# RoPE on half of each head: the load behind the first store waits for a point in VectorE's work

## The chip, the core and the metric

The kernel runs on one core of a Trainium2 chip. The metric is the device time of one execution in microseconds (us), as the median of several. A profile gives a second figure, the span: from the first to the last of the program's own instructions. The device time is longer than the span (162.1 against 160.3 us in the profiled run of the kernel before).

All runs told of here are fast, with a granted clock of 1.0. A ratio of two kernels is the mean time of one kernel's fast runs over the mean of the other's fast runs of the same rounds; it is therefore not quite the ratio of the medians that are quoted beside it.

## The reference

The input `x` is 16 x 512 x 16 x 64 in fp32, 33.55 MB. The first 32 of each head's 64 values are rotated with `cos` and `sin`; the other 32 pass through.

```python
x1, x2 = (x[..., :half_dim].copy(), x[..., half_dim:].copy())
...
rotated_first = x1[..., :half_dim // 2] * cos[..., :half_dim // 2] - x1[..., half_dim // 2:] * sin[..., :half_dim // 2]
rotated_second = x1[..., :half_dim // 2] * sin[..., :half_dim // 2] + x1[..., half_dim // 2:] * cos[..., :half_dim // 2]
return np.concatenate([rotated_first, rotated_second, x2], axis=-1).astype(np.float32)
```

All 33.55 MB have to be read and written once. That makes 67.1 MB of traffic.

## The kernel before

The data are cut into four tiles of 8.39 MB, each 128 partitions by 16 rows of 1024 values. Three tiles fit in a ring of three slots, so tile 3 reuses tile 0's slot. All large loads and stores go through one queue, that of SyncE (the sync queue). VectorE rotates a tile in place, in two halves of eight rows (`KC = 8`), each with two multiplications, a subtraction and an addition. The products with `sin` stand in PSUM, in one buffer of eight rows.

```python
load(0)
load(1)
load(2, 0, KC)
# ... the table of cos and sin is built ...

def rotate(t, lo, hi):
    # ... views of the tile and of the table ...
    nc.vector.tensor_mul(out=b_t, in0=x1, in1=s)
    nc.vector.tensor_mul(out=x1, in0=x1, in1=c)
    nc.vector.tensor_sub(...)
    nc.vector.tensor_add(...)

def turn(t):
    rotate(t, 0, KC)
    rotate(t, KC, K)
    return store(t)

turn(0)
load(2, KC, K)           # "the load behind the first store"
near = load(3, 0, KL)    # slot of tile 0: waits for store 0 to land
load(3, KL, K)
# ... store(1), from turn(1), is made to wait for `near` ...
turn(2)
turn(3)
```

The order at the DMA engines is: tile 0 in, tile 1 in, half of tile 2 in, store 0, the other half of tile 2 in, tile 3 in, stores 1, 2 and 3. In the profile these nine land in this order, at 22.96, 42.99, 52.76, 72.45, 81.94, 101.36, 120.72, 140.01 and 159.29 us (each on the last of the 16 engines).

Of the kernel before, what the change touches and what calls it, by code (L numbers as in the profile page):

```python
# [1 line left out]

# [4 lines left out]


@with_exitstack
def kernel(  # L10
    ctx: ExitStack,
    tc: tile.TileContext,
    x: bass.AP,
    cos: bass.AP,
    sin: bass.AP,
    out: bass.AP,
):
    nc = tc.nc
    fp32 = mybir.dt.float32
    P = 128  # L20
    B, S, H, D = x.shape
    Q = D // 4
    HF = D // 2



    K = 16
    T = B * S // (P * K)
    PB = S // K
    REP = P // PB  # L30
    R = H * D
    NS = 3
    KC = K // 2
    KL = 14

    xf = x.rearrange("b s h d -> (b s h d)").rearrange("(t p f) -> t p f", t=T, p=P)
    of = out.rearrange("b s h d -> (b s h d)").rearrange("(t p f) -> t p f", t=T, p=P)
    cosf = cos.rearrange("(p k) j -> p (k j)", k=K)
    sinf = sin.rearrange("(p k) j -> p (k j)", k=K)

    const_pool = ctx.enter_context(tc.tile_pool(name="const", bufs=1))
    b_pool = ctx.enter_context(tc.tile_pool(name="bp", bufs=1, space=bass.MemoryType.PSUM))


    ring = const_pool.tile([P, NS, K, H, D], fp32)
    stage = const_pool.tile([P, 2, K, HF], fp32)
    spun = const_pool.tile([P, 2 * K, Q], fp32)
    packed = const_pool.tile([PB, 2 * K, Q], fp32)
    table = const_pool.tile([P, 2, K, 2, Q], fp32)

    def rows(t, lo, hi):
        return ring[:, t % NS, lo:hi].rearrange("p k h d -> p (k h d)")

    def load(t, lo=0, hi=K):
        return nc.sync.dma_start(out=rows(t, lo, hi), in_=xf[t, :, lo * R : hi * R])

    def store(t, lo=0, hi=K):
        return nc.sync.dma_start(out=of[t, :, lo * R : hi * R], in_=rows(t, lo, hi))


    nc.vector.memset(stage[:, :, :, 0:Q], 0.0)  # L61
    spread = stage.rearrange("(j b) t k i -> j b t (k i)", b=REP)
    nc.gpsimd.dma_start(out=spread[:, 0, 0], in_=cosf)  # L63
    nc.gpsimd.dma_start(out=spread[:, 0, 1], in_=sinf)  # L64
# [7 lines that stand above are left out]
    PQ = PB // REP  # L72
    nc.vector.stream_shuffle(  # L73
        out=spun[:],
        in_=stage.rearrange("p t k j -> p (t k) j")[:, :, 0:Q],
        mask=[j % PQ * REP for j in range(PB)],
    )
    for q in reversed(range(REP)):
        n = PQ * (q + 1)
        nc.vector.tensor_copy(out=packed[0:n], in_=spun[q * PB : q * PB + n])  # L80

    for r in range(REP):
        nc.vector.tensor_copy(  # L83
            out=table[r * PB : (r + 1) * PB].rearrange("p t k c j -> p (t k) c j"),
            in_=packed.unsqueeze(2).to_broadcast((PB, 2 * K, 2, Q)),
        )
    C = table[:, 0].rearrange("p k c j -> p k (c j)")
    Sn = table[:, 1].rearrange("p k c j -> p k (c j)")

    def rotate(t, lo, hi):  # L90
        x1 = ring[:, t % NS, lo:hi, :, 0:HF]
        c = C[:, lo:hi].unsqueeze(2).to_broadcast((P, hi - lo, H, HF))
        s = Sn[:, lo:hi].unsqueeze(2).to_broadcast((P, hi - lo, H, HF))
        b_full = b_pool.tile([P, KC, H, HF], fp32, name="b_t")
        b_t = b_full[:, 0 : hi - lo]
        nc.vector.tensor_mul(out=b_t, in0=x1, in1=s)  # L96
        nc.vector.tensor_mul(out=x1, in0=x1, in1=c)  # L97
        nc.vector.tensor_sub(  # L98
            out=x1[:, :, :, 0:Q], in0=x1[:, :, :, 0:Q], in1=b_t[:, :, :, Q:HF]
        )  # L100
        nc.vector.tensor_add(  # L101
            out=x1[:, :, :, Q:HF], in0=x1[:, :, :, Q:HF], in1=b_t[:, :, :, 0:Q]
        )

    def turn(t):
        rotate(t, 0, KC)
        rotate(t, KC, K)
        return store(t)

    turn(0)  # L110
    load(2, KC, K)
    near = load(3, 0, KL)
    load(3, KL, K)

    tc.add_manual_dep(
        turn(1).ins,
        near.ins.name,
        mybir.DependencyInfo(mybir.DependencyClass.Sync, mybir.DependencyReason.DATA),
        reason="the store follows the loads at the DMA engines",
    )  # L120
    turn(2)
    turn(3)


# [1 line left out]
_INS = ['x', 'cos', 'sin']  # L126
_OUTS = [((16, 512, 16, 64), 'float32')]


# [23 lines left out]
```

## Time and profile before

| | before |
|---|---|
| device time, median of the first 3 runs | 161.58 us (161.43 to 161.9) |
| device time of the profiled run | 162.1 us |
| span of the profiled run | 160.3 us |
| bytes through the sync queue | 67.11 MB |
| VectorE busy | 112.4 us |

The prediction shows the windows of this profile, one for each transfer, and how to read them. In short: the DMA engines are never without work after the start (DMA share 0.99 to 1.02 in every stage from 22.1 us on), VectorE has slack (busy 112.4 of 160.3 us, none of it in the last stage).

### The profile page before, as it was taken

The numbers are of one execution on the slowest core, as the hardware profiler recorded it, in microseconds if no ns is written. First come the engines' busy times: TensorE is split into PE (matmuls) and PEld (weight loads), VectorE is DVE, ScalarE is ACT, GpSimd is POOL, SyncE is SP. The second block draws the span as 40 slices with busy tenths as digits, with TensorE's granted clock in tenths as the row PEclk, the third lists the DMA queues.
The fourth block names the chain that finished last, engine by engine and source line by source line (L and its number), as shares of the span: only waits on it lengthen the run. The fifth ranks groups of instructions, "written<-read, shape, count | busy, mean of one in ns | idle before, by whom it ended". The sixth has DMA issues, their size and how long they took to land.

```text
span 160.3 us, 113 instructions
## 1 busy us (share of the span) xinstructions
DVE 112.4 (70%) x43; POOL 1.4 (1%) x6
## 2 busy tenths in 40 slices
DVE  1000959999999999999999999999999950000000
POOL 3000000000000000000000000000000000000000
DMA  7969969699699996999999995996996996996990
GB/s 262 540 262 540 491 294 523 278 507 491 294 392 441 474 523 262 523 392 392 499 482 458 458 444 253 546 523 262 523 523 262 523 507 278 523 507 278 523 507 16
DMA packets 1504, 67.24 MB, mean 419 GB/s; under 512 B 192, under 2 KB 192, under 8 KB 224
## 3 DMA queue, kind: packets, MB, share of 16 engines
q1 hardware_dynamic: 1440, 67.11, 97.6%
q0 software_dynamic: 64, 0.13, 0.2%
HBM read 33.69 MB, written 33.55 MB: 419 GB/s over the span
## 4 chain that ended last, share of the span: by engine, by line
DVE 59%; DMA 14%; issue 7%; DVEq 1%
DVE b_t L96 22%; DVE ring L97 22%; DMA ring<-in_x_dram 14%; DVE ring L101 10%; DVE ring L98 4%; DVEq L148 1%; DVEq L96 0%
## 5 line engine op out<-in xcount | busy, mean ns | idle before, releaser
L96 DVE TENSOR_TENSOR b_t<-ring,table 128x4096 f32<-128x4096 f32 x8 | 35.5, 4432 | 2.1 <-DMA ring<-in_x_dram 1.9
L97 DVE TENSOR_TENSOR ring<-ring,table 128x4096 f32<-128x4096 f32 x8 | 35.4, 4424 | 0.3
L98 DVE TENSOR_TENSOR ring<-ring,b_t 128x2048 f32<-128x2048 f32 x8 | 18.3, 2287 | 0.3
L101 DVE TENSOR_TENSOR ring<-ring,b_t 128x2048 f32<-128x2048 f32 x8 | 18.2, 2280 | 0.0
L73 DVE LOAD_MASK_SELECT spun<-stage x1 | 0.0, 14 | 14.4 <-DMA stage<-in_sin_dram 14.4
L83 DVE COPY table<-packed 32x1024 f32<-32x1024 f32 x4 | 2.7, 684 | 0.1
L80 DVE COPY packed<-spun 32x512 f32<-32x512 f32 (+3 forms) x4 | 1.7, 416 | 0.1
L61 DVE MEMSET stage<- 128x512 f32 x1 | 0.5, 485 | 0.9 <-PEq L137 0.9
L73 DVE STREAM_SHUFFLE spun<-stage 128x512 f32<-128x512 f32 x1 | 0.7, 723 | 0.0
L63 POOL DMA_DIRECT2D stage<-in_cos_dram x1 | 0.6, 649 | 1.3 <-DVE stage L61 1.3
L64 POOL DMA_DIRECT2D stage<-in_sin_dram x1 | 0.5, 532 | 0.0
L137 POOL MEMSET const-float32-0.0<- 128x1 f32 x1 | 0.1, 93 | 0.2 <-issue 0.2
L137 POOL MEMSET const-bfloat16-1.0<- 128x1 bf16 x1 | 0.1, 95 | 0.0
L137 POOL MEMSET const-uint8-127<- 128x1 uint8 x1 | 0.1, 93 | 0.0
L137 POOL MEMSET const-float32-1.0<- 128x1 f32 x1 | 0.1, 92 | 0.0
## 6 DMA issues: line engine op xcount, KB each, us to landing
ring<-in_x_dram SPq DMA_DIRECT2D x2, 4096.0 KB, 41.4
ring<-in_x_dram SPq DMA_DIRECT2D x1, 7168.0 KB, 26.4
ring<-in_x_dram SPq DMA_DIRECT2D x1, 1024.0 KB, 28.5
stage<-in_cos_dram POOLq DMA_DIRECT2D x1, 64.0 KB, 9.0
stage<-in_sin_dram POOLq DMA_DIRECT2D x1, 64.0 KB, 13.4
out_dram<-ring SPq DMA_DIRECT2D x4, 25.6
ring<-in_x_dram SPq DMA_DIRECT2D x2, 32.0
```

What stands on the lines that cost most here:

```text
L61: nc.vector.memset(stage[:, :, :, 0:Q], 0.0)
L63: nc.gpsimd.dma_start(out=spread[:, 0, 0], in_=cosf)
L64: nc.gpsimd.dma_start(out=spread[:, 0, 1], in_=sinf)
L73: nc.vector.stream_shuffle(out=spun[:], in_=stage.rearrange("p t k j -> p (t k) j")[:, :, 0:Q], mask=[j % PQ * REP for j in range(PB)],)
L80: nc.vector.tensor_copy(out=packed[0:n], in_=spun[q * PB : q * PB + n])
L83: nc.vector.tensor_copy(out=table[r * PB : (r + 1) * PB].rearrange("p t k c j -> p (t k) c j"), in_=packed.unsqueeze(2).to_broadcast((PB, ...
L96: nc.vector.tensor_mul(out=b_t, in0=x1, in1=s)
L97: nc.vector.tensor_mul(out=x1, in0=x1, in1=c)
L98: nc.vector.tensor_sub(out=x1[:, :, :, 0:Q], in0=x1[:, :, :, 0:Q], in1=b_t[:, :, :, Q:HF])
L101: nc.vector.tensor_add(out=x1[:, :, :, Q:HF], in0=x1[:, :, :, Q:HF], in1=b_t[:, :, :, 0:Q])
L137: nc = _bacc.Bacc("TRN2", target_bir_lowering=False, num_devices=1)
L148: with _tile.TileContext(nc) as tc:
```

## The change

Behind store 0 the kernel issues the load of tile 2's second half. In the kernel before that load stands in the queue for 21 us while store 0 runs. The change issues it only near the store's end, by making it wait for VectorE to finish 11 of tile 1's 16 rows. To have a point at the right time, tile 1 is rotated in pieces of 6, 5 and 5 rows instead of 8 and 8. The other transfers keep their order and their waits.

```diff
-    turn(0)
-    load(2, KC, K)
-    near = load(3, 0, KL)
-    load(3, KL, K)
-    ...   # turn(1), its store waiting for `near`
-    turn(2)
-    turn(3)
+    rotate(0, 0, KC)
+    rotate(0, KC, K)
+    store(0)
+    rest = load(2, KC, K)
+    near = load(3, 0, KL)
+    load(3, KL, K)
+    rotate(1, 0, 6)
+    behind(rest, rotate(1, 6, 11))     # behind(): one more semaphore wait
+    rotate(1, 11, K)
+    behind(store(1), near)
+    for t in range(2, T):
+        rotate(t, 0, KC)
+        rotate(t, KC, K)
+        store(t)
```

(`rotate` now also returns its last instruction, so that a wait can name it.)

More of the change, by code (lines that the diff above doesn't have):

```diff
@@ L100, in rotate, with behind @@
         )
-        nc.vector.tensor_add(
+        return nc.vector.tensor_add(
             out=x1[:, :, :, Q:HF], in0=x1[:, :, :, Q:HF], in1=b_t[:, :, :, 0:Q]
         )
-    def turn(t):
+    def behind(transfer, point):
+        tc.add_manual_dep(
+            transfer.ins,
+            point.ins.name,
+            mybir.DependencyInfo(
+                mybir.DependencyClass.Sync, mybir.DependencyReason.DATA
+            ),
+            reason="issue the transfer near the end of the one in front of it",
+        )
+    rotate(0, 0, KC)
[9 more added lines that the diff above has]
+    for t in range(2, T):
         rotate(t, 0, KC)
         rotate(t, KC, K)
-        return store(t)
-    turn(0)
-    load(2, KC, K)
-    near = load(3, 0, KL)
-    load(3, KL, K)
-    tc.add_manual_dep(
-        turn(1).ins,
-        near.ins.name,
-        mybir.DependencyInfo(mybir.DependencyClass.Sync, mybir.DependencyReason.DATA),
-        reason="the store follows the loads at the DMA engines",
-    )
-    turn(2)
-    turn(3)
+        store(t)
 _INS = ['x', 'cos', 'sin']
```

## The prediction

> **What bounds the kernel now.** I read the page first, then the windows cut at the transfers' ends, then the issues and the sync queue's own waits, and last the timeline around the first store. The page, parts 1 and 3:
>
> ```profile
> DVE 112.4 (70%) x43; POOL 1.4 (1%) x6
> ...
> q1 hardware_dynamic: 1440, 67.11, 97.6%
> ```
>
> VectorE works 112.4 of 160.3 us; the sync queue's transfers fill 97.6% of what 16 DMA engines could do in the span. 67.11 MB is four tiles of 8.39 MB in and four out. The chain on the page is led by VectorE, but its last VectorE operation ends at 130.6 us and 28 us of pure storing follow, so I do not follow that chain: the DMA engines set the time. The windows, one for each stage of the traffic (tile 0 in; tile 1 in; first half of tile 2 in; store 0; second half of tile 2 in; tile 3 in; stores 1, 2, 3), with columns stretch, length, busy times, clock, DMA share, GB/s:
>
> ```profile
> 0.74:22.10 21.36, 5.62 (x11) 1.18 (x2) 1.00 0.95 399
> 22.10:42.30 20.20, 19.11 (x6) 0.00 (x0) 1.00 1.00 417
> 42.30:52.10 9.80, 9.73 (x4) 0.00 (x0) 1.00 1.01 431
> 52.10:71.40 19.30, 19.16 (x6) 0.00 (x0) 1.00 0.99 431
> 71.40:81.10 9.70, 9.63 (x4) 0.00 (x0) 1.00 1.02 438
> 81.10:100.46 19.36, 19.19 (x7) 0.00 (x0) 1.00 1.00 433
> 100.46:119.80 19.34, 19.20 (x7) 0.00 (x0) 1.00 1.02 441
> 119.80:139.10 19.30, 10.71 (x4) 0.00 (x0) 1.00 0.99 428
> 139.10:158.41 19.31, 0.00 (x0) 0.00 (x0) 1.00 0.99 431
> ```
>
> The reader is to see that transfers follow one another without a hole, and that from 52.1 us on each 8.39 MB takes 19.3 us, whether it is a load or a store and whether or not something is queued behind it. (A packet is counted whole where it starts, so single figures scatter by some GB/s around the true rate.) The rate is lower only before 52.1: the start costs about 2 us and tile 1's load runs at 417.
>
> Now the place of the change. The issues view, cut to the moment of the first store and of the load behind it (last column: us from issue to landing):
>
> ```profile
> ring<-in_x_dram SPq DMA_DIRECT2D x1, 4096.0 KB, 31.6
> out_dram<-ring SPq DMA_DIRECT2D x1, 22.5
> ```
>
> The store is issued at 49.94 and lands at 72.4; the load is issued at 50.33 and lands at 81.9, that is 9.5 us after the store, its own 4.19 MB at 441 GB/s. So they do not share the engines by turns: the load stands in line for 21 us and then runs. The sync queue's own waits, in the window from 49 to 75 us:
>
> ```profile
> SPq L58 <- DVE ring L101: 26.9, 1, 26.9
> SPq L55 <- DMA out_dram<-ring: 21.7, 1, 21.7
> ```
>
> The first is store 0 waiting for tile 0's rotation. The second is tile 3's load, which reuses tile 0's slot and so waits for store 0's landing. In these 21.7 us the sync queue has nothing to do: the new wait falls inside it.
>
> [...]
>
> **The change, part by part.** The order of instructions on the sync queue is the same; the load of tile 2's second half gets one more wait, on VectorE. VectorE does tile 1 in three pieces in place of two: 12 instructions instead of 8.
>
> *VectorE's added cost.* The work is split, not enlarged[...]. Tile 1 ends at 77.5 instead of 76.83, and the last rotation at 131.3 instead of 130.6. None of it reaches the end: store 1 waits for tile 3's load to land (98.8); store 2, issued at 103.7, would be issued at 104.4, and its turn comes at 119.8; store 3, issued at 131.3, has its turn at 139.1. The smallest slack is 7.8 us. Cost on the path: 0.
>
> *The point of issue.* From the timeline:
>
> ```profile
> 49.94 4.43 DVE L96 TENSOR_TENSOR b_t<-ring,table 128x4096 f32<-128x4096 f32 x1
> ...
> 63.39 4.43 DVE L96 TENSOR_TENSOR b_t<-ring,table 128x4096 f32<-128x4096 f32 x1
> ```
>
> Eight rows of tile 1 take 13.45 us, of which 13.42 are its four instructions. [...] With 0.03 each for gaps the first piece ends at 60.2 and the second at 68.86. The load is then issued at about 68.9 instead of 50.33. Store 0's data end at 71.4, so the load is 2.5 us early.
>
> *Is 2.5 us enough?* Windows at the first load of all and at the hand-over:
>
> ```profile
> 0.74:1.70 0.96, 0.48 (x1) 0.00 (x0) 1.00 0.00 0
> 1.70:2.70 1.00, 0.00 (x0) 1.00 (x2) 1.00 3.06 1049
> ...
> 68.80:69.80 1.00, 1.00 (x1) 0.00 (x0) 1.00 2.42 1049
> 69.80:71.30 1.50, 1.50 (x1) 0.00 (x0) 1.00 0.00 0
> 71.30:72.30 1.00, 0.98 (x1) 0.00 (x0) 1.00 1.22 524
> ```
>
> The first load was issued at 0.74; its packets started between 1.7 and 2.7 on all engines (1.05 MB, 16 packets of 64 KB), so 1 to 2 us from issue to work on a cold queue. The store's last 16 packets start between 68.8 and 69.8, and the load's first ones after 71.3. Issued at 68.9, the load is ready by 69.9 to 70.9, 0.4 to 1.4 us ahead of need: no hole, cost 0. Its landing stays at 81.9, 8.4 us before VectorE asks for it (90.28 in the timeline). Tile 3's load is still issued at store 0's landing, 72.5.
>
> *What could be gained.* If one transfer's waiting descriptors slow the one in front, store 0 should run below the stores that have nothing at their end. It does not: 19.30 us, against 19.34, 19.30 and 19.31. [...] All that is before 52.1 lies ahead of the point where the change begins.
>
> Sum: [...]0 for VectorE, 0 for the hand-over: 161.6 us, within the noise of the three runs before (161.43 to 161.9).
>
> **Rivals.** *A: a hole at the hand-over.* If queue start-up in mid-stream takes over 2.5 us, or the load's reads can no longer begin under the store's last writes, the engines stand idle. The cold start cost 1 us of no packets, and stage one took 21.4 us against 19.3, about 2 us over. For it: the lead is a single packet's time[...]. Against it: 2.5 us exceeds the cold start's 1 to 2[...]. It would make 162.0 to 163.5. I give it one chance in eight.
>
> *B: the queued load slows the store, so its delay helps.* For it: the change's author applies the same idea already to store 1, which waits for tile 3's load; and tile 1's load, with another behind it, ran at 417. Against it: tile 0's load had two behind it and store 0 one, and store 0 runs at full rate; tile 3's load had a further load behind it and took 19.4 with that. [...]
>
> *C: VectorE becomes the bound.* It gets 0.7 us later, against a slack of 7.8 us. It would need eleven times the cost. 161.6 unless that arithmetic is badly off.
>
> *D: the sync queue blocks.* It stands before the load until 68.9, where it stood before the next one until 72.5 in any case. Nothing else is issued between, so 161.6.
>
> **Range and chances.** The centre is the sum, 161.6. [...]upward the spread and the mild half of A, 162.3. Two per cent is 3.2 us. [...]slower by that would need a hole longer than the whole cold start. So 0.01, 0.97 and 0.02.
>
> **What would show each step right or wrong.** In the changed kernel the sync queue should wait for VectorE's line 101-equivalent a second time, about 18.5 us; the load's issue should stand near 68.9 and its time to landing fall from 31.6 to about 13.0 us; store 0's stay near 22.5; tile 3's load wait some 3 us for the store in place of 21.7; VectorE's busy time rise by 0.6 to about 113.0 us. In the windows, the stage of store 0 should still be 19.3 us and the next one start at once at 71.4. A stretch without packets between 71.4 and 72.4, with the landing later than 82, would be rival A. Store 0 landing 0.3 us or more earlier with everything behind it moved along would be B. I would be wrong altogether if the transfers before 52.1 changed, since nothing of the change reaches them by this reading.

The sum came to 161.6 us, with a range of 161.1 to 162.3.

What the traces give:

- The five full-tile stages after 52.1 us ran at 431, 433, 441, 428 and 431 GB/s, 433 in the mean. A 64 KB packet took 2.42 us in the median.
- Tile 3's load, which waits for store 0, was issued at 72.47 us, 0.02 us after the store's last landing (72.45). So the shown start of that issue is the end of its wait.
- The load's first packet starts at 71.40 us, while the store's last one runs to 71.78: the two overlap.
- An estimate, made from this profile after the fact: operations of 4096 elements a partition took 4.432 and 4.424 us, those of 2048 took 2.287 and 2.280. A straight line through their means has 1.047 ns for an element and 139 ns for an instruction, so four instructions more add 0.56 us. By the same estimate six rows take 10.21 us and five 8.60, and the point is reached at 68.81 us. In the changed kernel the two pieces took 10.24 and 8.64 us and the point was reached at 68.76 (the first piece began 0.06 us earlier).

## The result, and the profile after

| | before | changed |
|---|---|---|
| device time, median of 6 runs | 161.58 us (161.43 to 162.16) | 162.25 us (162.16 to 162.57) |
| ratio | 1 | 1.0036 (95%: 1.0019 to 1.0054) |
| span, profiled run | 160.3 us | 160.0 us |
| device time, profiled run | 162.1 us | 162.16 us |

The changed kernel is slower by 0.36%: 0.67 us between the medians. That counts as the same at the 2% mark, and lies in the predicted range, but it is clear of the noise and was not expected. And the two profiles seem to say the contrary: the changed kernel's span is shorter. So the first task is to find where 0.67 us can hide.

The page of the changed kernel, its head and VectorE's line:

```profile
span 160.0 us, 117 instructions
## 1 busy us (share of the span) xinstructions
DVE 112.9 (71%) x47; POOL 1.4 (1%) x6
```

VectorE has four instructions more and is busy 0.5 us longer (112.9 against 112.4; 0.6 was foreseen). The sync queue's own waits between 49 and 75 us (who waited for whom, total, times, longest):

```profile
SPq L58 <- DVE ring L101: 26.9, 1, 26.9
SPq L55 <- DVE ring L101: 18.5, 1, 18.5
SPq L55 <- DMA out_dram<-ring: 2.6, 1, 2.6
```

The new wait is the second line. The third is tile 3's load, which still waits for store 0 to land, but now for 2.6 us, where it was 21.7: the queue's waiting has only changed its name. The timeline gives the issue, and the issues view the time from issue to landing:

```profile
68.76 3.77 SPq L55 DMA_DIRECT2D ring<-in_x_dram  x3
```

```profile
ring<-in_x_dram SPq DMA_DIRECT2D x1, 4096.0 KB, 12.9
```

The load was issued at 68.76 and landed 12.9 us later, as foreseen (68.9 and 13.0). The windows of the changed kernel, one for each transfer as in the prediction (stretch, length, VectorE, GpSimd, clock, DMA share, GB/s):

```profile
22.00:41.35 19.35, 18.22 (x6) 0.00 (x0) 1.00 1.00 432
41.35:51.10 9.75, 9.68 (x4) 0.00 (x0) 1.00 1.01 434
51.10:70.42 19.32, 19.11 (x9) 0.00 (x0) 1.00 1.00 433
70.42:80.60 10.18, 10.08 (x5) 0.00 (x0) 1.00 1.02 414
80.60:99.98 19.38, 19.21 (x7) 0.00 (x0) 1.00 0.99 428
```

Two stages differ from the first profile of the kernel before. Tile 1's load (first line) took 19.35 us at 432 GB/s, where it had taken 20.20 at 417: 0.85 us won in a stage that ends long before the change begins. And the moved load (fourth line) took 10.18 us at 414, where it had taken 9.70 at 438: 0.48 us lost. The first lies ahead of all that the change touches, so it may be one run's chance; the second may be the change. This had to be tested, and so had the difference between device time and span: 2.16 us here, 1.8 before.

### The profile page after: what moved, and what is told of

The parts are those of the page before. It is cut to its first block, busy times and chain, and to the rows that moved or that the text cites. A ratio compares the mean times of both kernels' runs of the same rounds, so it can differ in the third digit from the quotient of the medians.

```text
span 160.0 us, 117 instructions
## 1 busy us (share of the span) xinstructions
DVE 112.9 (71%) x47; POOL 1.4 (1%) x6
## 4 chain that ended last, share of the span: by engine, by line
DVE 60%; DMA 14%; issue 7%; DVEq 1%
DVE b_t L96 22%; DVE ring L97 22%; DMA ring<-in_x_dram 14%; DVE ring L101 10%; DVE ring L98 5%; DVEq L156 1%; DVEq L96 0%
## 5 line engine op out<-in xcount | busy, mean ns | idle before, releaser
L96 DVE TENSOR_TENSOR b_t<-ring,table 128x4096 f32<-128x4096 f32 (+2 forms) x9 | 35.6, 3958 | 2.1 <-DMA ring<-in_x_dram 1.9
L97 DVE TENSOR_TENSOR ring<-ring,table 128x4096 f32<-128x4096 f32 (+2 forms) x9 | 35.6, 3950 | 0.3
L98 DVE TENSOR_TENSOR ring<-ring,b_t 128x2048 f32<-128x2048 f32 (+2 forms) x9 | 18.4, 2050 | 0.3
L101 DVE TENSOR_TENSOR ring<-ring,b_t 128x2048 f32<-128x2048 f32 (+2 forms) x9 | 18.4, 2042 | 0.0
```

The source lines that it names most:

```text
L98: nc.vector.tensor_sub(out=x1[:, :, :, 0:Q], in0=x1[:, :, :, 0:Q], in1=b_t[:, :, :, Q:HF])
L101: return nc.vector.tensor_add(out=x1[:, :, :, Q:HF], in0=x1[:, :, :, Q:HF], in1=b_t[:, :, :, 0:Q])
```

## The experiments

All twelve were correct and ran in three groups, with five rounds each beside the kernel before, which gave four to six fast runs of each kernel. Each group has its own controls; their median span was 159.8 us in all three. This table sums them up. "Span" is the median over all fast runs of that kernel. "Beyond" is the median of device time minus span. "Tail" is, in the profile, the span minus the landing of the last store (its issue plus its time to landing). "Last landing" is the median span less the tail: the end of the data traffic.

| kernel | device time | ratio | span | beyond | tail | last landing |
|---|---|---|---|---|---|---|
| before_again | 161.49 | 0.9992 | 159.7 | 1.80 | 1.04 | 158.7 |
| after_again | 162.21 | 1.0040 | 160.0 | 2.2 | 1.04 | 159.0 |
| split_no_wait | 161.97 | 1.0023 | 159.8 | 2.2 | 1.04 | 158.8 |
| wait_at_8_rows | 161.53 | 0.9999 | 159.75 | 1.8 | 1.04 | 158.7 |
| tiny4 | 161.90 | 1.0022 | 159.7 | 2.15 | 1.04 | 158.7 |
| wait_at_10_rows | 161.97 | 1.0024 | 159.8 | 2.2 | 1.04 | 158.8 |
| wait_at_12_rows | 163.08 | 1.0099 | 160.85 | 2.2 | 1.04 | 159.8 |
| tile3_later | 162.16 | 1.0038 | 160.4 | 1.8 | 1.35 | 159.05 |
| after_tiny4 | 162.21 | 1.0039 | 160.4 | 1.8 | 1.35 | 159.05 |
| tiny8 | 161.82 | 1.0018 | 160.1 | 1.8 | 1.35 | 158.75 |
| wait_at_mul | 161.75 | 1.0007 | 160.0 | 1.8 | 1.04 | 159.0 |
| head_early | 162.14 | 1.0036 | 159.9 | 2.2 | 1.1 | 158.8 |

Spans are recorded to 0.1 us, so differences of 0.1 in the last column mean nothing. The 95% intervals of the ratios are about 0.0013 wide on either side.

### The two kernels once more

`before_again` and `after_again` are the two kernels without an edit.

> The kernel before, unchanged, for a second profile and for the noise of a ratio. Every theory expects a ratio of 1.000 within 0.002. The point is the profile: in the first one tile 1's load ran at 417 GB/s (20.2 us), where in the changed kernel it took 19.35 us at 432. If that slowness belongs to the kernel before, it is there again (20.2 us); if it comes and goes by the run, this profile may show 19.4 us and a span some 0.8 us shorter than 160.3.

> The changed kernel, unchanged, in the same rounds as its controls. Every theory expects a ratio of about 1.004 (162.2 us). In the profile the stage of the load behind the first store should again take about 10.2 us in place of 9.7, if the lost half microsecond there is the kernel's and not that one run's.

Measured: 161.49 and 162.21 us, ratios 0.9992 and 1.0040. The difference is the kernel's. In the second profile of the changed kernel the moved load takes as long as in the first (10.18 us there):

```profile
70.49:80.75 10.26, 10.16 (x5) 0.00 (x0) 1.00 1.02 409
```

The windows of the second profile of the kernel before (tile 1 in, half of tile 2 in, store 0, the load behind it):

```profile
22.10:41.45 19.35, 18.23 (x6) 0.00 (x0) 1.00 1.00 435
41.45:51.15 9.70, 9.63 (x4) 0.00 (x0) 1.00 1.01 436
51.15:70.78 19.63, 19.49 (x6) 0.00 (x0) 1.00 1.00 426
70.78:80.62 9.84, 9.77 (x4) 0.00 (x0) 1.00 0.99 423
```

Tile 1's load took 19.35 us this time, so its slowness was one run's. (What slowed it stays open. One of the 11 control runs of the kernel before in this group took 162.12 us against 161.53 in the median, so such an execution is not unique, though that one has no trace.) And now store 0 and the load behind it, 19.63 and 9.84, take 0.47 us more than in the first profile (19.30 and 9.70). (These windows are cut where the first of the 16 DMA engines starts a transfer. To the landing on the last engine, 0.02 us after which the load that waits for store 0 was issued in the first profile, the second profile is only 0.15 us longer: 29.33 us from the landing of tile 2's first half to that of its second, against 29.18.) The kernel before, too, has slow packets where the store hands over to the load; the first profile happened to have none.

### Which part of the change costs: the split or the wait?

`split_no_wait`, from the changed kernel:

```diff
-    behind(rest, rotate(1, 6, 11))
+    rotate(1, 6, 11)
```

> Tile 1 in 6, 5 and 5 rows, without the new wait. Theory H (the load is issued too near the store's end, so its first packets run slowly at the hand-over): as before, ratio 1.000 within 0.002, the load's stage 9.7 us. Rival V (VectorE's 0.6 us of added work reaches the end): ratio 1.004.

`wait_at_8_rows`, from the changed kernel:

```diff
-    rotate(1, 0, 6)
-    behind(rest, rotate(1, 6, 11))
-    rotate(1, 11, K)
+    behind(rest, rotate(1, 0, KC))
+    rotate(1, KC, K)
```

> Tile 1 in two halves as before, with the wait, at the end of the first half: the load is issued at about 63.4 us, some 7 us before the store's data end. Theory H: 7 us is enough, ratio 1.000 within 0.002, stage 9.7 us. Rival W (a wait there costs in itself, whatever its point, through the sync queue or an added semaphore): ratio 1.004.

The wait without the split costs nothing (0.9999). That rules out rival W, a wait that costs in itself. The split without the wait costs 0.4 us (1.0023): theory H had expected 1.000 and missed. But its last store does not land later (158.8 against 158.7). So rival V, which has the longer chain of VectorE reach the end, is wrong as well: the time is lost after the span. Device time minus span is about 2.2 in every run of the changed kernel and of `split_no_wait`, and about 1.8 in every run of the kernel before and of `wait_at_8_rows`, which have the old number of instructions. What is there to see after the span? The DMA queues of `split_no_wait` between 159 and 165 us have one line:

```profile
q14 instruction: 1, 0.01, 0.5%
```

It is one packet of the queue that the profile names "instruction". In the trace it starts 1.7 us after the span's end. The first profile of the changed kernel has one as well: 8,192 bytes, started at 161.69 us and 0.42 us long. The kernel before and `wait_at_8_rows` have no packet at all there. In the first profiles of both kernels this queue's other 13 packets all start before the span. Hence theory F: the four instructions bring one more such packet at the very end, and the device time counts it. This is a guess at the cause; what makes the packet come is not shown.

### Is it the number of instructions?

`tiny4`, and with 8 in place of 4 `tiny8`, from the kernel before:

```diff
+    for _ in range(4):
+        nc.vector.memset(stage[:, :, 0:1, 0:1], 0.0)
     nc.vector.memset(stage[:, :, :, 0:Q], 0.0)
```

> The kernel before with four memsets of 2 elements a partition more on VectorE, at its start where it is idle. Tile 1 stays in halves, no new wait. Theory F (four more VectorE instructions bring one more 8 KB instruction fetch after the program's span, which the device time counts): span as before (159.8), device time minus span 2.18 in place of 1.79, so 161.9 us, ratio 1.0024, and a packet of the instruction queue after the span. Rival V (the 0.37 us of the split without a wait come from VectorE's longer work on tile 1): 161.5, ratio 1.000.

> The kernel before with eight tiny memsets more. Theory F: difference 1.79 and span 159.8, so 161.5, ratio 1.000, where four such memsets gave 1.0022. If each instruction costs: 162.3, ratio 1.0044.

`after_tiny4` is the same edit of four memsets in the changed kernel.

> The changed kernel with four tiny memsets more on VectorE at its idle start: eight instructions more than the kernel before, as in tile3_later, where the last instruction fetch came 0.33 us after the span instead of 1.7 us and the device time minus span was 1.79. Theory F (the place of that fetch, not the number of instructions as such, costs 0.39 us): difference back at 1.79, span still 160.0, device time 161.8, ratio 1.0016, so a longer program is 0.4 us faster than the changed kernel. If each instruction costs: 2.5 and 162.6.

`tiny4` met the expectation: 1.0022, the span unchanged, 2.15 us beyond, and the packet 1.7 us after the span. Four instructions at a time when VectorE is idle cost as much as the split (ratios 1.0022 and 1.0023). So the split's cost is that of a longer VectorE program and has nothing to do with tile 1.

The two with eight instructions more missed: 1.0018 where theory F in its second form (the later position is free) had 1.000, and 1.0039 where it had 1.0016. Beyond the span they are at 1.8 again, as expected, but the tail inside the span has grown from 1.04 to 1.35 us. The trace shows where. At the end each engine has a closing DRAIN instruction (the views call VectorE's "DVEq"). These lines are of `tiny4` and of `tiny8`, each from 158 us on; they give its shortest, median and longest time in ns and its first and last start in us:

```profile
L150 DVEq DRAIN  x1: 19/19/19, 159.3 to 159.3; - x1
```

```profile
L150 DVEq DRAIN  x1: 125/125/125, 159.8 to 159.8; - x1
```

With eight instructions more, VectorE's DRAIN starts 0.4 us later (1.01 instead of 0.58 us after the last landing), with GpSimd's closing instructions behind it (in the first profile of the kernel before, GpSimd's next one starts 0.02 us after VectorE's DRAIN has ended). The packet starts 0.5 us after that DRAIN has ended, 0.3 us after the last of the program's instructions. So the delay has not become free, it has moved into the span; and VectorE is not waiting for that packet, which has not begun when it goes on. But the cost does not grow with the number either: 0.3 to 0.4 us for four as for eight. What is shown: four instructions or eight more on VectorE than in the kernel before cost 0.3 to 0.4 us at the end of the execution, once, and a packet of the instruction queue appears there; with eight, the time is lost on VectorE, ahead of the packet. What holds VectorE is not shown, and with four the delay lies behind the span, where no instruction is on record. So theory F stays a guess.

### How near to the store's end may the load be issued?

Four kernels move the point, `wait_at_8_rows` among them. From the changed kernel, `wait_at_10_rows` and `wait_at_12_rows`:

```diff
-    rotate(1, 0, 6)
-    behind(rest, rotate(1, 6, 11))
-    rotate(1, 11, K)
+    rotate(1, 0, 5)                     # 12 rows: 0, 7
+    behind(rest, rotate(1, 5, 10))      # 12 rows: 7, 12
+    rotate(1, 10, K)                    # 12 rows: 12, K
```

> Tile 1 in 5, 5 and 6 rows, wait after 10 rows: the load is issued at about 67.1 us, 1.7 us earlier than in the changed kernel. Difference of device time and span 2.18 (theory F). Theory H (the nearness to the store's end costs about 0.25 us of span at 68.8): part or all of it comes back, span 159.8 to 159.9, device time 162.0. Rival J (the issues of tile 3's load at 71.7, during the load's first packets, cause the loss, whatever the point): span 160.05, 162.2.

> Tile 1 in 7, 5 and 4 rows, wait after 12 rows: the load is issued at about 70.4 us, just at the end of the store's data. Theory H: its packets start 1 to 2 us after the issue, so a hole of 0.5 to 1.5 us and slow first packets: span 160.8 to 161.8, device time 163.0 to 164.0. Rival J: tile 3's load is issued at the store's landing as before, so the loss does not grow beyond the hole itself, 0.5 to 1 us less than under H.

`wait_at_mul` is the changed kernel with tile 1 in two halves, the load waiting for the first multiplication of the second half (`rotate` returns its first instruction):

```diff
-    rotate(1, 0, 6)
-    behind(rest, rotate(1, 6, 11))
-    rotate(1, 11, K)
+    rotate(1, 0, KC)
+    behind(rest, rotate(1, KC, K))
```

> Tile 1 in two halves as before, no instruction more; the load waits for the first multiplication of the second half, so it is issued at about 67.9 us, 0.9 us ahead of the changed kernel's point. This is the idea of the change without its split. Theory F: difference 1.79. Theory H: at 67.5 the span was 159.8 and at 68.8 160.0, so 159.8 to 160.0 here and 161.6 to 161.8, ratio 1.0005 to 1.0015. For this to beat the kernel before, the span would have to fall below 159.7.

All three met what theory H expected: 161.97, 163.08 and 161.75 us. By the point of issue, with the time from the end of the issue to the store's landing (the wait of tile 3's load for the store, from the sync queue's waits), the hand-over (in the trace, from the landing of tile 2's first half to that of its second) and the last landing from the table above:

| kernel | issue | left to the store's landing | hand-over | last landing |
|---|---|---|---|---|
| before_again | 50.35 | 21.0 | 29.33 | 158.7 |
| wait_at_8_rows | 63.37 | 8.0 | 29.35 | 158.7 |
| wait_at_10_rows | 67.47 | 4.0 | 29.30 | 158.8 |
| wait_at_mul | 67.82 | 3.5 | 29.51 | 159.0 |
| changed (after_again) | 68.92 | 2.3 | 29.74 | 159.0 |
| wait_at_12_rows | 70.67 | 0.6 | 30.40 | 159.8 |

Up to some 4 us before the landing nothing is lost. At 2.3 us 0.3 to 0.4 are lost, at 0.6 us 1.1. `wait_at_mul` lies between in its one trace, but its ratio of 1.0007 (0.9994 to 1.0020) can't be told from 1, so where between 4.0 and 2.3 us the loss sets in stays open; it adds no instruction and has no cost beyond the span. None of the points is better than having the load in the queue all along, so no version came out of this that beats the kernel before.

What happens at the hand-over shows in windows cut at the packets. (A packet is counted where it starts.) First, in the kernel before (second profile), the last packets of store 0, then the first two packets of the load on each engine, then the third:

```profile
68.00:70.76 2.76, 2.76 (x1) 0.00 (x0) 1.00 1.00 380
70.76:73.35 2.59, 2.56 (x2) 0.00 (x0) 1.00 0.97 405
73.35:75.77 2.42, 2.42 (x2) 0.00 (x0) 1.00 1.00 433
```

The same in the changed kernel:

```profile
67.98:70.40 2.42, 2.38 (x2) 0.00 (x0) 1.00 1.00 433
70.40:73.29 2.89, 2.86 (x2) 0.00 (x0) 1.00 1.05 363
73.29:75.70 2.41, 2.38 (x2) 0.00 (x0) 1.00 1.01 435
```

And with the load issued at 70.67, the store's last packets with what follows up to the first start of the load, and the load's first packets:

```profile
68.00:71.62 3.62, 3.59 (x3) 0.00 (x0) 1.00 0.67 290
71.62:73.46 1.84, 1.80 (x2) 0.00 (x0) 1.00 0.93 285
```

With the load in the queue, the store's last packets are slow (380 GB/s) and the load's first ones nearly at full pace. In the changed kernel the store ends at full pace (433), and the load's first two packets are slow instead (363). So the late issue does what its author may have had in mind, it frees the store's end; but the load pays for it. In the traces, the time that these packets take over their usual 2.42 us (64 KB) or 1.21 (32 KB) sums to 0.40 us in the mean over the 16 engines for the kernel before (second profile) and to 0.62 for the changed one.

That mean is not the cost, though. In `wait_at_10_rows` it is 0.83 us, and the hand-over is no longer (29.30). What seems to count is which engines are slow. With the load in the queue, the engines that are ahead lose the most: in `wait_at_10_rows` they land tile 2's first half 0.83 us apart and its second half 0.25 us apart, in the kernel before (second profile) 0.50 and 0.43. In the changed kernel they drift apart instead: from 0.44 to 0.70 us in the first profile and from 0.58 to 0.75 in the second. The distance stays up to the last store (0.67 to 0.71 us at each of the six landings from there on in the first profile, 0.68 at the last), and the execution ends with the last engine: that landing is at 158.94 us, and the sync queue's closing wait ends at 158.96. The hand-over to that engine's landing takes 29.69 and 29.74 us in the two profiles of the changed kernel, against 29.33, which matches the 0.3 us of the last landing. With the issue at 70.67 a real hole comes on top: 16 packets in 3.62 us, where they need 2.42.

The first profile of the kernel before is an exception that stays open: the load was in the queue, and none of these packets was slow. In the other traces with the load queued 8 us or more before the landing (`before_again`, `split_no_wait`, `wait_at_8_rows`, `tiny4`, `tiny8`) the store's last packet took 0.24 to 0.47 us too long in the mean; in those of the changed kernel, `after_tiny4` and `tile3_later`, 0.03 at most.

### Is it the late issue itself, or the issues behind it?

In the changed kernel tile 3's load is issued at 71.7, just while the moved load has its slow first packets (rival J). `tile3_later`, from the changed kernel:

```diff
     behind(rest, rotate(1, 6, 11))
-    rotate(1, 11, K)
+    behind(near, rotate(1, 11, 14))
+    rotate(1, 14, K)
```

> The changed kernel with tile 1 in 6, 5, 3 and 2 rows, and tile 3's load held back until 14 rows are done (about 74.3 us instead of 71.7), so that nothing is issued while the load behind the store has its first packets; 74.3 is still 6 us ahead of its turn. Theory H: span as in the changed kernel, 160.0 to 160.1, the load's first two packets on each engine slow as there. Rival J: the slow packets vanish, span 159.8. Difference of device time and span 2.18 or more (eight instructions more than before).

Tile 3's load was issued at 74.33. The expected time beyond the span (2.18 or more) was missed, for the reason above. The last landing stayed late, 159.05 against 159.0, and in the trace the moved load's first packets were as slow as before. The span alone (160.4) would have misled here: 0.3 of it are the longer tail of a program with eight instructions more. Rival J falls.

`head_early`, from the changed kernel, keeps a piece of the load in the queue:

```diff
-    rest = load(2, KC, K)
+    load(2, KC, KC + 1)
+    rest = load(2, KC + 1, K)
```

> The changed kernel with the first of the load's eight rows issued right behind the store, without the wait, and the other seven with it at 68.8. Theory H (the load's first packets are slow because nothing of it was queued while the store's last packets ran): they are at full pace again, span 159.8, and the store's last packets are slowed instead, as in the kernel before (0.33 us in the mean over the engines). If what counts is when the bulk is issued: span 160.0, store's last packets at full pace. Device time minus span is not foreseen here: the sync queue has one instruction more.

Its windows, for the store's last packets, the 0.5 MB of the head, and the first packets of the other seven rows:

```profile
67.90:70.57 2.67, 2.63 (x2) 0.00 (x0) 1.00 1.00 393
70.57:71.82 1.25, 1.22 (x2) 0.00 (x0) 1.00 0.85 347
71.82:74.10 2.28, 2.28 (x1) 0.00 (x0) 1.00 1.09 442
```

The store's last packets are slow again (393, in the kernel before 380), and the last landing is back at 158.8, although seven eighths of the load are issued at 68.59. (The 347 of the middle line counts only those of the head's packets that start in the stretch; some engines reach them later. In the trace most of the head's 4 KB packets took 0.16 us, which is 26 GB/s an engine, against 27 for a 64 KB packet of 2.42 us.) So, in this trace, it is having something of the load in the queue while the store's last packets run that decides which packets are slow. (The head also has smaller packets than the load had; this run alone doesn't separate the two.) The gain in time is weaker: the hand-over took 29.48 us in this trace, between the kernel before and the changed one. Beyond the span this kernel stayed at 2.2, so that its ratio, 1.0036, is no better than that of the changed kernel: the gain at the hand-over was not to be seen against the span's scatter and a tail of 1.1.

## Why the prediction was right and wrong

**The bound.** Right. The DMA engines set the time, and in all twelve runs the last landing followed the hand-over, never VectorE's rotations.

**VectorE's added cost.** The forecast was right: busy 112.9 us (113.0 foreseen), the point reached at 68.76 (68.86), and no effect on the path, as `split_no_wait` shows with its last landing at 158.8. But the step "0 for VectorE" counted the instructions' time alone. That four more instructions lengthen the program, and that this alone costs 0.3 to 0.4 us after the span, was missing from the sum altogether. `tiny4` measures it: 0.34 us between the medians (161.90 against the controls' 161.56), and 2.15 against 1.8 us beyond the span. It is about half of the slowdown. The 1.8 us between the first profile's span and its device time were on the table, and the working never asked what they hold.

**"Issued at 68.9, the load is ready ... no hole, cost 0."** This step failed. There was no hole, but the load's first packets were slow, and the last landing came 0.3 us later. The working compared the 2.5 us of lead with the 1 to 2 us until packets *start*; what counts, by the table of points, is how long before the store's landing the load is in the queue: 4.0 us ahead lost nothing, 2.3 us ahead 0.3 to 0.4. Its first packets then ran at 363 GB/s, against 405 with the load queued all along. Rival A came nearest in its second half ("can no longer begin under the store's last writes"), though the traces show slow packets and not what slows them; its size, 0.4 to 1.9 us, was too large for a lead of 2.5 us. `wait_at_12_rows` shows A's first half as well: hole and slow packets together, 1.1 us.

**"What could be gained ... store 0 runs at full rate."** Wrong for an ordinary run. It was read from one profile of an execution that took 162.1 us. In the second profile the store's last packets are slow, as in four other traces with the load queued, by 0.24 to 0.47 us. So rival B was dismissed on a reading that does not hold: with a load waiting, the store's end is usually slow. Freeing it gains nothing, though, because the load then pays.

**Rivals C and D** fell as foreseen.

**The sum.** 0.3 us at the hand-over and 0.4 after the span make 0.7 against 0.72 measured between the medians of `after_again` and `before_again` (162.21 and 161.49). The prediction had 0. That 162.25 lay below the range's upper end of 162.3 was luck: the room had been made for the mild half of rival A, and half of the loss came from a term that was not in the sum.

## What to carry to other kernels

In this kernel a load that follows a store in a full queue (DMA share 0.99 to 1.02) lost nothing measurable when it was issued 4.0 us before the store's landing, 0.3 to 0.4 us at 2.3, and 1.1 us at 0.6. Holding it back to spare the store only moved the slow packets to the load: the store's last ones rose from 380 to 433 GB/s, the load's first ones fell from 405 to 363. When an effect of half a per cent is at stake, look at a second profile of the same kernel before reading a stage from the first, compare landings rather than spans, and count also what lies between the span and the device time: here four more instructions on VectorE, in tile 1 or at its idle start, cost there what no stage shows (2.2 us in place of 1.8).
